# A hybrid encoder layer on one core: two backward states per step at the projection's end, and chunks beside the memory on the memory's PSUM banks

## The chip, the cores and the metric

The kernel runs on one core of one Trainium2 chip. The metric is the device time in microseconds (us) from start to end of one execution. A core has a TensorE (PE, matrix products into PSUM), a VectorE (DVE), a ScalarE (ACT), a GpSimd (POOL) and a SyncE (SP, which here issues most of the DMA loads); each works through its own queue in order, and semaphores tie the queues together.

## What is computed

One encoder layer in float32 for a sequence of 2048 rows of 1024 features, with 256 rows of memory:

```python
u = RMSNorm(x);  P = u @ w_in                 # one input projection
# Hyena group, 512 channels: short convolution, then two gated long convolutions
z = x1 * (h1 * z + d1 z);  z = x2 * (h2 * z + d2 z)      # filters as long as the sequence
# mLSTM group, 4 heads of 128: one scan forwards, one backwards, in chunks
s = (q @ k.T) * w;  num = s @ v + inter * (q @ C);  den = sum(s) + inter * (q @ n)
y += num / maximum(abs(den), exp(-m));  C = decay * C + (we * k).T @ v   # n likewise
x = x + concat(group_norm(z), group_norm(sigmoid(o) * y)) @ w_out
x = x + cross_attention(RMSNorm(x), RMSNorm(mem), wq, wk, wv, wo)        # 4 heads
x = x + relu(RMSNorm(x) @ w1) ** 2 @ w2;  return RMSNorm(x)
```

## The kernel before, in words

**Products.** The large products are three matmuls each on rounded parts of the operands: high by high, low by high and high by low (`mm3`, lines L355, L358, L359); `split` (L366) makes the parts with an ACT cast and a DVE subtraction. PSUM has eight banks of 2 KB per partition. Four carry the tag `mm` (method `mm`, L161) and take turns, four the tag `hy` (method `hy`, L164). A product that wants a bank waits until whoever read the bank four turns earlier has finished.

**The order.** The program is written as Python generators, each yielding a rough cost; `weave(a, b, wa, wb)` steps two generators so that their costs keep a ratio, `paced` and `among` put steps of one between steps of another. A scheduler, which simulates the engines, then decides the order of instructions on each engine; what it may reorder depends on data and on the turns of banks and buffers. So the written order, the set of banks and the buffers together set the queues.

**Stages.** First come the filters of the long convolution and the input projection (column sweeps `sweep`, row tiles `natural`), then the projection's rest woven with the convolution (`p.hyena`). Beside the projection's end run the mLSTM's gates and its *backward states*: the backward scan needs, for each of 16 chunks of 128 rows, the state that the later chunks leave, so `states`/`backward` walks from the last chunk to the first and stores the 15 states to memory (`cbd`). One step loads k and v (`L1178`, `L1184`), weights v, and in `update` (L1188) makes four matmuls (two to each of two banks, L1200) that DVE adds to the decayed old state (L1206).

The last stretch of the projection is `among(chain(sweep, natural), back, 1)`: one backward state after each step, and the remaining ones without anything between them.

Then follows the stage on which the change works, `chain(p.turned_in(), take(n, 1), beside_each(n, take(m, 5)))`:

- `n` is `memproj` (L693), the attention's work on the memory. `project` (L708) makes, for each of eight pairs, 16 products of the normed memory with a 256-column block of a weight; ACT copies the result to `kt` (L710). Then `keys` (L725, pairs 1 to 4) or `values` (L737, pairs 5 to 8) multiply it with a block of the next weight (16 or 8 products), ACT copies each bank to a buffer `o` and POOL's queue stores it (`gd`, `vw`). The weights `wm` come through SP (L415).
- `m` is `mlstm` (L1227). Its first step sets up and loads chunks 0 and 1, its next four are chunks 0 to 3. A chunk takes four score products (L1284, one bank), masks on POOL, an exponential on ACT (L1293) and a product on DVE (L1294); then for each direction eight products in two banks `pn` (L1322 with v, L1324 with the forward state `cf` or the stored backward state `cbn`), whose results ACT (L1327, L1336) and DVE (L1338) turn into the output `ht`; then `update` of the forward state. After every second chunk `bank_rsqrt` (L205) takes an inverse root on a PSUM bank with Newton steps (L213), which L1356 applies to the two chunks' rows. The other 12 chunks run later, woven into the attention.

The last part of the convolution also falls into this stage. For each of eight blocks SP loads transformed rows (`a<-zg`, two loads, L339) and the gate's rows (`a<-hy`, four loads, L974); PE makes the inverse transform's products (L173, L186), and the gated, normed rows are stored (`yh<-a`). The products of the transform before it are L987.

The *attention* stage starts with the loads of the mixed rows (`wn<-yh`, L1473), 16 transposes (L1479), a split, and the output projection (first matmul L355 with `act`) with columns of `w_out` (L1405).

In the generators the five steps of the mLSTM stand one behind each pair's step of the memory:

Of the kernel before, what the change touches and what calls it, by code (L numbers as in the profile page):

```python
# [128 lines left out]
class Prog:  # L129
    def __init__(self, ctx, tc, a):  # L130
        self.tc, self.nc, self.a = tc, tc.nc, a
        nc = self.nc
        self.ctx = ctx
        self.dr = ctx.enter_context(tc.tile_pool(name="dr", bufs=1, space=DRAM))
        self.s = {}
        cp = self.cp = ctx.enter_context(tc.tile_pool(name="cp", bufs=1))
        ident = cp.tile([128, 128], F32, name="ident")
        nc.gpsimd.memset(ident, 1.0)
        nc.gpsimd.affine_select(ident, ident, pattern=[[-1, 128]], compare_op=ALU.is_equal, fill=0.0,
                                base=0, channel_multiplier=1)  # L140
        self.ident = ident
        self.eps = cp.tile([128, 1], F32, name="eps")
        nc.vector.memset(self.eps, EPS)
        self.ones = cp.tile([128, 128], F32, name="ones")
        nc.vector.memset(self.ones, 1.0)
        self.flip = 0
        self.banks, self.strict = [], False
        self.pending = []
        self.prepq = None
        self.hooks, self.made, self.lag, self.rowb = {}, 0, [], None  # L150
        self.rbp = cp.tile([128, 16], F32, name="rbp")
        self.fb = cp.tile([128, 8], F32, name="fb")
        nc.scalar.activation(self.fb[:, 4:5], self.eps, AF.Copy)
        par = self.par = cp.tile([128, 192], F32, name="par")
        nc.scalar.dma_start(out=par, in_=a["par"])
        self.g_mix, self.g_mem, self.gx, self.gf = (par[:, 8 * i:8 * i + 8] for i in range(4))
        self.cw = par[:, 32:92].rearrange("p (i c) -> p i c", i=3)
        self.cb, self.gb = par[:, 92:112], par[:, 112:128]
        self.ps = ctx.enter_context(tc.tile_pool(name="ps", bufs=1, space=PSUM))
# [4 lines left out]
    def hy(self):  # L164
        t = self.ps.tile([128, 512], F32, tag="hy", name="hy", bufs=4)
        self.banks.append(t[:, 0:1].tensor.name)
        return t

    def beside(self, *products, pin=False):
        names = [p[0].tensor.name for p in products]  # L170
# [31 lines left out]
        else:  # L202
            self.nc.vector.tensor_copy(out, in_)

    def bank_rsqrt(self, pool, ss, n):  # L205
        nc, c = self.nc, ss.shape[1]
        m, ys = (pool.tile([128, c], F32, tag="br" + x, name="br" + x, bufs=2) for x in "my")
        nc.scalar.activation(m, ss, AF.Identity, bias=self.eps, scale=1.0 / n)
        b = self.hy()
        y, t = b[:, 0:c], b[:, 16:16 + c]  # L210
        nc.vector.tensor_scalar(y.bitcast(I32), m.bitcast(I32), -0.5, float(0x5F3759DF), ALU.mult, ALU.add)
        for _ in range(3):
            nc.vector.tensor_copy(ys, y)  # L213
            nc.vector.tensor_tensor(t, y, ys, ALU.mult)
            nc.vector.scalar_tensor_tensor(t, t, -0.5, m, ALU.mult, ALU.mult)
            nc.vector.scalar_tensor_tensor(y, t, 1.5, ys, ALU.add, ALU.mult)
        return y
# [970 lines left out]
    def update(self, sb, new, old, kk, va, r, eng, pin=None, bufs=2):  # L1188
        nc, pin = self.nc, pin or (lambda i: i)
        WC, DC = self.gcols[:, 2], self.gcols[:, 3]  # L1190
        ve = sb.tile([128, 4, 129], F32, tag="ve", name="ve", bufs=bufs) if bufs > 1 else va
        if eng is nc.scalar:
            for h in range(4):
                eng.activation(ve[:, h], va[:, h], AF.Copy, scale=WC[:, r + h:r + h + 1])
        else:
            eng.tensor_tensor(ve, va, WC[:, r:r + 4].unsqueeze(2).broadcast_to([128, 4, 129]), ALU.mult)
        for p in range(2):
            pc = self.hy()
            for i in range(2):
                pin(nc.tensor.matmul(pc[:, 129 * i:129 * i + 129], kk[:, 2 * p + i], ve[:, 2 * p + i], start=True, stop=True))  # L1200
            if old is None:
                nc.vector.tensor_copy(new[:, 2 * p:2 * p + 2].rearrange("d h e -> d (h e)"), pc[:, 0:258])
                continue
            for i in range(2):
                h = 2 * p + i
                nc.vector.scalar_tensor_tensor(new[:, h], old[:, h], DC[:, r + h:r + h + 1],  # L1206
                                               pc[:, 129 * i:129 * i + 129], ALU.mult, ALU.add)
# [19 lines left out]
    def mlstm(self, es):  # L1227
# [51 lines left out]

        def scores(n, ld):  # L1280
            qn, kk_t, cbn, va, rows_ = ld
            sp = self.hy().rearrange("p (h t) -> p h t", h=4)
            for h in range(4):
                nc.tensor.matmul(sp[:, h], kk_t[:, h], qn[:, h], start=True, stop=True)  # L1284
            for d in range(2):
                r = 64 * d + 4 * n
                nm = rows_[d, 0]
                if (d, 1) in rows_:
                    it = rows_[d, 1]
                    nc.gpsimd.tensor_tensor(it, it, qn, ALU.mult)  # L1290
                nc.gpsimd.tensor_tensor(nm, nm, masks[d].unsqueeze(1).broadcast_to([128, 4, 128]), ALU.add)
                for h in range(4):
                    nc.scalar.activation(nm[:, h], nm[:, h], AF.Exp, bias=GC[:, r + h:r + h + 1])  # L1293
                nc.vector.tensor_tensor(nm, nm, sp, ALU.mult)  # L1294
# [4 lines left out]
        for n in range(16):  # L1299
# [10 lines left out]
            for d in range(2):  # L1310
                r = 64 * d + 4 * n
                nm = rows_[d, 0]
                state = cf if d == 0 else cbn
                if d == 0:
                    y = sb.tile([128, 4, 128], F32, tag="h0", name="ht", bufs=2)
                pvs = []
                for p in range(2):
                    pn = self.hy()
                    for i in range(2):
                        h = 2 * p + i  # L1320
                        dst = pn[:, 129 * i:129 * i + 129]
                        nc.tensor.matmul(dst, nm[:, h], va[:, h], start=True, stop=state is None)  # L1322
                        if state is not None:
                            nc.tensor.matmul(dst, rows_[d, 1][:, h], state[:, h], start=False, stop=True)  # L1324
                    pvs.append(pn[:, 0:258].rearrange("t (h e) -> t h e", h=2))
                for p, pv in enumerate(pvs):
                    nc.scalar.activation(pn[:, 260 + 2 * p:262 + 2 * p].unsqueeze(2), pv[:, :, 128:129], AF.Abs)  # L1327
                den = sb.tile([128, 4, 1], F32, tag="den", name="den", bufs=4)
                dv = den.rearrange("t h o -> t (h o)")
                nc.vector.tensor_tensor(dv, pn[:, 260:264], EC[:, r:r + 4], ALU.max)  # L1330
                nc.vector.reciprocal(dv, dv)
                for p, pv in enumerate(pvs):
                    for i in range(2):
                        h = 2 * p + i
                        if d == 0:
                            nc.scalar.activation(y[:, h], pv[:, i, 0:128], AF.Copy, scale=dv[:, h:h + 1])  # L1336
                            continue
                        nc.vector.scalar_tensor_tensor(y[:, h], pv[:, i, 0:128], dv[:, h:h + 1], y[:, h], ALU.mult, ALU.add)  # L1338
# [10 lines left out]
                nc.scalar.activation(junk[:, h], y[:, h], AF.Square, accum_out=ss[:, c:c + 1])  # L1349
            ys.append(y)  # L1350
            if n % 2:
                rv = self.bank_rsqrt(sb, ss, 128)
                for i, y in enumerate(ys):
                    t0 = 128 * (n - 1 + i)
                    for h in range(4):
# [744 lines left out]
def program(p):  # L2100
    with ExitStack() as ms:
        with ExitStack() as es:
# [15 lines left out]
            with ExitStack() as hs:  # L2118
# [1 line left out]
                             p.natural(0, (3,)),  # L2120
                             paced(chain(p.sweep((4, 5, 8, 9), 0, False), p.natural(0, (0, 1))),
                                   p.gates(), back := p.states(), (0, 1) * 6 + (2,) * 6 + (2, 0)),
                             among(chain(p.sweep((6, 7), 0, False), p.natural(0, (2,), p.prep_mem, 2)), back, 1),
                             )
                weave(rest, p.hyena(hs), 445, 329)
            for _ in chain(p.turned_in(), take(n, 1), beside_each(n, take(m, 5))):
                pass
        with ExitStack() as rs:
            p.ts = rs.enter_context(ExitStack())
            p.tail_open(p.ts)  # L2130
# [10 lines left out]
def among(g, h, every):  # L2141
    for i, v in enumerate(g):
        yield v
        if i % every == every - 1:
            next(h, None)
    for _ in h:
        pass


def paced(g, h1, h2, plan):  # L2150
    for v, n in zip(g, plan):
        yield v
        if n:
            next((h1, h2)[n - 1], None)
    yield from g


def beside_each(g, h):
# [43 lines left out]
```

## Time and profile before

| | us |
|---|---|
| median of 3 runs | 3063.18 |
| lowest and highest run | 3056.71, 3065.72 |
| the profiled execution's own time | 3063.97 |
| its span in the profile | 3062.3 |
| PE busy | 2979.0 |
| DVE busy | 1953.2 |
| ACT busy | 1491.5 |
| POOL busy | 1263.4 |
| data moved by DMA | 607.03 MB, mean 198 GB/s |

The span is the time from the first to the last recorded instruction; the own time of the execution also holds what lies around it. Engine names and line numbers in the profile's rows are those of the kernel before. In a row of the timeline stand the start, the length, the engine, the line, the operation with output and input, the shape, the count, and in brackets the idle time just before with what ended it. Windows rows give the busy time of each engine in a stretch and the granted clock of PE. The mean granted clock over the whole span is 0.989.

### The profile page before, as it was taken

The numbers are of one execution on the slowest core, as the hardware profiler recorded it, in microseconds if no ns is written. First come the engines' busy times: TensorE is split into PE (matmuls) and PEld (weight loads), VectorE is DVE, ScalarE is ACT, GpSimd is POOL, SyncE is SP. The second block draws the span as 40 slices with busy tenths as digits, with TensorE's granted clock in tenths as the row PEclk, the third lists the DMA queues.
The fourth block names the chain that finished last, engine by engine and source line by source line (L and its number), as shares of the span: only waits on it lengthen the run. The fifth ranks groups of instructions, "written<-read, shape, count | busy, mean of one in ns | idle before, by whom it ended". The sixth has DMA issues, their size and how long they took to land.

```text
span 3062.3 us, 44144 instructions
## 1 busy us (share of the span) xinstructions
PE 2979.0 (97%) x14799; PEld 2367.6 (77%) x14799; DVE 1953.2 (64%) x3442; ACT 1491.5 (49%) x2930; POOL 1263.4 (41%) x1025
## 2 busy tenths in 40 slices
PE   9999999998999989999999999999999999999998
PEld 7666667775678867888888888888888888888876
DVE  8855464557755447867665666558555686566695
ACT  6443455634664235555544455556555543333335
POOL 0112113321443654333223247765665374344653
PEclk9999999999999999999999999999999999999999
DMA  6655676686877976463567466657544555444434
GB/s 223 197 186 170 213 263 214 192 273 216 279 229 221 348 265 198 149 228 125 196 202 264 137 219 217 208 178 250 190 151 152 196 192 169 118 157 121 155 103 165
DMA packets 423644, 607.03 MB, mean 198 GB/s; under 512 B 36847, under 2 KB 229999, under 8 KB 422393
## 3 DMA queue, kind: packets, MB, share of 16 engines
q1 hardware_dynamic: 395972, 525.42, 53.6%
q0 software_dynamic: 18992, 62.96, 5.6%
q10 hardware_dynamic: 8452, 15.83, 1.4%
q8 instruction: 117, 1.92, 0.3%
q14 instruction: 111, 0.90, 0.1%
HBM read 401.67 MB, written 202.41 MB: 197 GB/s over the span
## 4 chain that ended last, share of the span: by engine, by line
PE 58%; DVE 2%; DMA 1%; issue 1%; ACT 1%; POOL 0%; SPq 0%; DVEq 0%; POOLq 0%; ACTq 0%
PE mm L355 12%; PE mm L359 12%; PE mm L358 12%; PE hy L355 6%; PE hy L359 6%; PE hy L358 6%; PE hy L1322 1%; PE hy L1324 1%; DVE bl L1693 0%; PE hy L1284 0%; PE hy L1596 0%; DVE acc L1991 0%; PE hy L1200 0%; PE hy L1479 0%; DVE acc L2028 0%
## 5 line engine op out<-in xcount | busy, mean ns | idle before, releaser
L1692 ACT CAST ah<-w 128x512 fp32r<-128x512 f32 x284 | 176.6, 623 | 303.8 <-PE hy L358 150.2
L1693 DVE TENSOR_TENSOR bl<-wr,bh 128x512 fp32r<-128x512 f32 x213 | 240.3, 1132 | 126.5 <-ACT bh L1692 126.2
L366 DVE TENSOR_TENSOR wl<-wn,wh 128x512 fp32r<-128x512 f32 (+1 forms) x296 | 220.0, 787 | 89.2 <-ACT wh L366 89.2
L355 PE MATMUL mm<-xh,wh 128*128 128x512 f32 x640 | 264.5, 415 | 2.3 <-ACT xh L366 1.1
L358 PE MATMUL mm<-xl,wh 128*128 128x512 f32 x640 | 255.9, 400 | 5.5 <-DVE xl L366 5.4
L359 PE MATMUL mm<-xh,wl 128*128 128x512 f32 x640 | 254.5, 398 | 0.0
L1692 ACT CAST bh<-wr 128x512 fp32r<-128x512 f32 x232 | 143.4, 621 | 227.9 <-PE mm L359 169.5
L1693 DVE TENSOR_TENSOR al<-w,ah 128x512 fp32r<-128x512 f32 x236 | 216.5, 918 | 57.2 <-ACT ah L1692 56.9
L359 PE MATMUL mm<-bh,al 128*128 128x512 f32 x576 | 223.8, 391 | 3.4 <-DVE al L1693 3.4
L355 PE MATMUL mm<-bh,ah 128*128 128x512 f32 x576 | 225.9, 392 | 1.3 <-DVE acc L1854 1.1
L358 PE MATMUL mm<-bl,ah 128*128 128x512 f32 x576 | 224.9, 390 | 0.0
L366 ACT CAST wh<-wn 128x512 fp32r<-128x512 f32 (+1 forms) x296 | 164.3, 620 | 102.6 <-PE mm L359 51.1
L358 PE MATMUL mm<-act,wh 128*128 128x512 f32 x512 | 202.0, 395 | 0.0
L359 PE MATMUL mm<-act,wl 128*128 128x512 f32 x512 | 199.9, 392 | 0.0
L355 PE MATMUL mm<-act,wh 128*128 128x512 f32 x512 | 199.0, 395 | 0.6 <-ACT wh L366 0.5
L355 PE MATMUL hy<-bh,ah 128*128 128x512 f32 x448 | 175.2, 391 | 0.0
L358 PE MATMUL hy<-bl,ah 128*128 128x512 f32 x448 | 174.6, 390 | 0.0
L359 PE MATMUL hy<-bh,al 128*128 128x512 f32 x448 | 174.4, 390 | 0.0
L331 POOL TENSOR_TENSOR b<-b 128x512 f32<-128x512 f32 x32 | 48.1, 1504 | 293.6 <-DVE b L330 277.4
L355 PEld LDWEIGHTS mm<-xh,wh 128*128 128x128 f32 x640 | 121.1, 190 | 52.4 <-issue 18.7
L358 PEld LDWEIGHTS mm<-xl,wh 128*128 128x128 f32 x640 | 121.2, 189 | 50.9 <-issue 19.1
L355 PE MATMUL mm<-wh,xh 128*128 128x256 f32 (+1 forms) x512 | 155.7, 304 | 1.8 <-DVE a L960 1.8
(396 smaller groups left out, 8257.4 us busy)
## 6 DMA issues: line engine op xcount, KB each, us to landing
wr<-hc SPq DMA_DIRECT2D x224, 256.0 KB
w<-in_ff_w_dram SPq DMA_DIRECT2D x172, 256.0 KB
hc<-wn SPq DMA_DIRECT2D x128, 256.0 KB
wn<-in_w_in_dram SPq DMA_DIRECT2D x100, 256.0 KB
hc<-q SPq DMA_DIRECT2D x96, 256.0 KB
fs<-a SPq DMA_DIRECT2D x32, 512.0 KB
zs<-a POOLq DMA_DIRECT2D x32, 512.0 KB, 6.6
a<-fs SPq DMA_DIRECT2D x64, 256.0 KB
```

Of the source, the lines that this page charges most:

```text
L331: nc.gpsimd.tensor_tensor(b, f, b, ALU.subtract)
L355: first = mm(ps, lh, rh, start=start, stop=False)
L358: mm(ps, lh, rl, start=False, stop=False)
L359: self.last = mm(ps, ll, rh, start=False, stop=stop)
L366: both = (self.nc.scalar.copy(hi, src), self.nc.vector.tensor_tensor(lo, src, hi.bitcast(F32), ALU.subtract))
L1322: nc.tensor.matmul(dst, nm[:, h], va[:, h], start=True, stop=state is None)
L1324: nc.tensor.matmul(dst, rows_[d, 1][:, h], state[:, h], start=False, stop=True)
L1692: self.nc.scalar.copy(hi, src)
L1693: eng.tensor_tensor(lo, src, hi.bitcast(F32), ALU.subtract)
```

## The change

Two things are edited. In the projection's last stretch, `twice(back)` lets each step make two backward states instead of one. And while a flag `early` is set, which is during the memory stage alone, the mLSTM's scores, products, updates and the bank of the norm come from `mm()`, the set that the memory's products and the projection use, instead of `hy()`, the set that the convolution uses. Later chunks, in the attention, use `hy()` as before. The backward states of the last stretch still use `hy()` where the flag is not set.

```diff
+    def spare(self):
+        return self.mm() if self.early else self.hy()
...
-    def bank_rsqrt(self, pool, ss, n):
+    def bank_rsqrt(self, pool, ss, n, bank=None):
...
-        b = self.hy()
+        b = bank or self.hy()
...
-            pc = self.hy()
+            pc = self.spare()
...
-            sp = self.hy().rearrange("p (h t) -> p h t", h=4)
+            sp = self.spare().rearrange("p (h t) -> p h t", h=4)
...
-                    pn = self.hy()
+                    pn = self.spare()
...
-                rv = self.bank_rsqrt(sb, ss, 128)
+                rv = self.bank_rsqrt(sb, ss, 128, self.spare())
...
-                             among(chain(p.sweep((6, 7), 0, False), p.natural(0, (2,), p.prep_mem, 2)), back, 1),
+                             among(chain(p.sweep((6, 7), 0, False), p.natural(0, (2,), p.prep_mem, 2)), twice(back), 1),
...
+            p.early = True
             for _ in chain(p.turned_in(), take(n, 1), beside_each(n, take(m, 5))):
                 pass
+            p.early = False
...
+def twice(g):
+    for v in g:
+        yield v + next(g, 0)
```

Lines of the changed kernel are four higher in this part than those of before: L708 becomes L712, L725 L729, L737 L741, L173 L177, L186 L190, L1200 L1204, L1284 L1288, L1322 and L1324 L1326 and L1328, L1479 L1483, L339 L343, L974 L978.

On PE, at the start of the memory stage, the order before had a backward state (L1200 with `va`) or a block of the convolution (L173, L186) in each pair of the memory:

```order
L708 MATMUL mm<-mt,wm 128x256 x3
L1200 MATMUL hy<-va,kn 128x129 x4
L708 MATMUL mm<-mt,wm 128x256 x25
L173 MATMUL hy<-a,e_2743 32x512
L186 MATMUL hy<-a,e_2743 32x512 x7
L708 MATMUL mm<-mt,wm 128x256 x4
L725 MATMUL mm<-kt,wm 128x256 x16
L708 MATMUL mm<-mt,wm 128x256 x11
L1200 MATMUL hy<-va,kn 128x129 x4
```

The changed order at the same place, the first two pairs of the memory and the scores of the first chunks (L1288):

```order
L712 MATMUL mm<-mt,wm 128x256 x26
L177 MATMUL hy<-a,e_2743 32x512
L190 MATMUL hy<-a,e_2743 32x512 x7
L712 MATMUL mm<-mt,wm 128x256 x6
L729 MATMUL mm<-kt,wm 128x256 x16
L1288 MATMUL mm<-qn,kk_t 128x128 x4
...
L712 MATMUL mm<-mt,wm 128x256 x14
L729 MATMUL mm<-kt,wm 128x256 x12
L177 MATMUL hy<-a,e_2743 32x512
L190 MATMUL hy<-a,e_2743 32x512 x7
L729 MATMUL mm<-kt,wm 128x256 x4
L177 MATMUL hy<-a,e_2743 32x512
```

The states have moved ahead of the stage. Of the convolution's eight blocks three now stand ahead of the memory's first matmul (before, two), four stand in its first two pairs, and the eighth stands in the update of chunk 0; before, the last one stood behind the fifth pair.

On PE, at the end of the memory stage, the order before had the last value products (L737), then chunks 2 and 3 with nothing between, of which the start is shown, and after them the attention's transposes:

```order
L737 MATMUL mm<-wm,kt 128x512 x3
L1200 MATMUL hy<-ve,kn 128x129 x4
L1284 MATMUL hy<-qn,kk_t 128x128 x4
L1322 MATMUL hy<-va,rw 128x129
L1324 MATMUL hy<-cf,rw 128x129
```

In the changed order chunk 3's update is followed by two more pairs of the memory, and then by the transposes:

```order
L1204 MATMUL mm<-ve,kn 128x129 x4
L712 MATMUL mm<-mt,wm 128x256 x16
L741 MATMUL mm<-wm,kt 128x512 x8
L712 MATMUL mm<-mt,wm 128x256 x16
L741 MATMUL mm<-wm,kt 128x512 x16
L1483 MATMUL hy<-ident,wn 128x128 x16
L1288 MATMUL hy<-qn,kk_t 128x128 x4
```

Chunks 1 to 3 stand whole between pairs of the memory, each as one piece of 4 scores, 16 products and 4 update products, where before matmuls of the memory stood inside the pieces of chunks 0 and 1.

On SP's queue, the last blocks of the convolution (`a<-zg`, `a<-hy`) before, among the memory's weights:

```order
L1258 DMA cbn<-cbd 128x516 x2
L415 DMA wm<-in_xa_wo_dram 128x1024 x2
L415 DMA wm<-in_xa_wv_dram 128x4x256 x2
L339 DMA a<-zg_2739 128x1024 x2
L974 DMA a<-hy 32x1024 x4
L415 DMA wm<-in_xa_wo_dram 128x1024 x2
L415 DMA wm<-in_xa_wv_dram 128x4x256 x2
```

The same place in the changed order:

```order
L343 DMA a<-zg_2739 128x1024 x2
L978 DMA a<-hy 32x1024 x4
L419 DMA wm<-in_xa_wk_dram 128x4x256 x2
L419 DMA wm<-in_xa_wq_t_dram 128x1024 x2
L1263 DMA qn<-qt 128x4x128
L1263 DMA kk_t<-kt 128x4x128
L343 DMA a<-zg_2739 128x1024 x2
L978 DMA a<-hy 32x1024 x4
L419 DMA wm<-in_xa_wv_dram 128x4x256 x2
L343 DMA a<-zg_2739 128x1024 x2
L978 DMA a<-hy 32x1024 x4
L419 DMA wm<-in_xa_wq_t_dram 128x1024 x2
```

Ahead of the last block's loads there now stand 16 of the memory's weight items (the `x` counts of L419 in the whole queue), before 26 (L415).

More of the change, by code (lines that the diff above doesn't have):

```diff
@@ L135, in __init__ @@
         self.s = {}
+        self.early = False
         cp = self.cp = ctx.enter_context(tc.tile_pool(name="cp", bufs=1))
```

## The prediction

> **What bounds the kernel now.** I read the page first: its span, the busy shares of the engines and the clock.
>
> ```profile
> span 3062.3 us, 44144 instructions
> PE 2979.0 (97%) x14799; PEld 2367.6 (77%) x14799; DVE 1953.2 (64%) x3442; ACT 1491.5 (49%) x2930; POOL 1263.4 (41%) x1025
> ```
>
> TensorE (PE) is busy for 97% of the span; whatever else the change does, it can only win where PE waits or runs at a lower clock. The profiled execution took 3063.97 us with a span of 3062.3 us, so 1.7 us lie around the span, and it is 0.8 us above the median of the three runs, 3063.18 us. I make the sum as a difference and add it to the median.
>
> Next I cut the span by the windows view. Its columns are the length, the busy time of PE, weight load, DVE, ACT and POOL (with instruction counts), the granted PE clock, the DMA share and GB/s. The first row reaches from the first matmul of the memory projection to the first matmul of the output projection: the stretch on which the change works.
>
> ```profile
> core 0: us, PE busy (x) PEld busy (x) DVE busy (x) ACT busy (x) POOL busy (x), PEclk, DMA share, GB/s
> 997.07:1170.91 173.84, 155.37 (x794) 120.64 (x793) 87.59 (x281) 65.96 (x200) 105.30 (x118) 0.93 0.86 289
> 1020.00:1030.00 10.00, 9.30 (x39) 8.04 (x40) 5.16 (x17) 2.72 (x7) 6.47 (x7) 0.83 1.02 376
> 1140.00:1150.00 10.00, 4.84 (x19) 4.27 (x20) 8.69 (x36) 2.60 (x11) 4.98 (x6) 0.51 0.47 161
> 1150.00:1160.00 10.00, 8.93 (x59) 8.38 (x58) 7.24 (x26) 6.38 (x28) 6.37 (x6) 0.81 0.52 158
> 1160.00:1170.00 10.00, 4.60 (x25) 4.12 (x25) 6.07 (x23) 7.50 (x24) 2.15 (x2) 0.71 0.52 159
> ```
>
> PE misses 173.84 − 155.37 = 18.5 us of 173.84, and the four ten-microsecond windows show a clock well below 1. The timeline of PE shows where it waits; the last bracket is the idle time and what ended it. These are all the waits of the stretch.
>
> ```profile
> 997.07 1.46 PE L708 MATMUL mm<-mt,wm 128*128 128x256 f32 x6
> 1020.70 3.68 PE L725 MATMUL mm<-kt,wm 128*128 128x256 f32 x8 [2.36 <-ACT kt L710]
> 1134.20 1.13 PE L1284 MATMUL hy<-qn,kk_t 128*128 128x128 f32 x8 [1.60 <-issue]
> 1142.23 0.77 PE L1322 MATMUL hy<-va,rw 128*128 128x129 f32 x2 [5.12 <-DVE bry L213]
> 1145.10 0.80 PE L1322 MATMUL hy<-va,rw 128*128 128x129 f32 x2 [0.81 <-DVE ht L1356]
> 1149.31 2.09 PE L1200 MATMUL hy<-ve,kn 128*128 128x129 f32 x8 [2.12 <-ACT ht L1336]
> 1157.48 1.23 PE L1200 MATMUL hy<-ve,kn 128*128 128x129 f32 x8 [0.36 <-ACT ht L1336]
> 1159.41 0.66 PE L1479 MATMUL hy<-ident,wn 128*128 128x128 f32 x4 [0.70 <-DVE cf L1206]
> 1160.38 1.29 PE L1479 MATMUL hy<-ident,wn 128*128 128x128 f32 x8 [0.32 <-issue]
> 1166.72 1.12 PE L1479 MATMUL hy<-ident,wn 128*128 128x128 f32 x4 [5.04 <-DVE act L366]
> 1170.91 1.18 PE L355 MATMUL mm<-act,wh 128*128 128x512 f32 x4
> ```
>
> The brackets add up to 18.4 us. The largest, 5.12 us, stands in chunk 2 of the mLSTM, which comes after the last memory matmul: chunks 2 and 3 run bare there, and the bank that chunk 2's product wants is held by the norm of chunks 0 and 1 (L213, L1356). The other large one, 5.04 us, is the entry to the attention stage, between transposes.
>
> **The change part by part.** *What it can remove.* The idle time is 18.4 us. The clock costs busy time × (1 − granted clock): 9.30 × 0.17 = 1.6, 4.84 × 0.49 = 2.4, 8.93 × 0.19 = 1.7, 4.60 × 0.29 = 1.3 us, together 7.0. So 25.4 us can go at most, if chunks 1 to 3 stand among memory products and nothing is late there.
>
> *Work that only moves.* By the order of the changed kernel, the three backward states still left beside the memory, and one more block of the convolution's last inverse transform, stand ahead of the first memory matmul.
>
> ```profile
> 1028.97 1.05 PE L1200 MATMUL hy<-va,kn 128*128 128x129 f32 x8
> 1086.18 0.61 PE L173 MATMUL hy<-a,e 64*32 64x512 f32 x1
> 1087.20 7.17 PE L708 MATMUL mm<-mt,wm 128*128 128x256 f32 x32
> 1094.21 7.03 PE L737 MATMUL mm<-wm,kt 128*128 128x512 f32 x16
> ```
>
> A state is 0.9 us of PE (its matmuls start at 1028.97, the next group at 1029.86 in the same view), so three are 2.7 us; a convolution block goes from 1086.18 to 1087.20, 1.0 us. In front of the memory they cost the same 3.7 us that they no longer cost behind, and memory starts near 1000.8. I cost this at nothing: the projection's products (mm banks) cover the states' VectorE work there. Without that cover it is at most three waits of a state's chain, which I put at 0 to 3 us, with the nearest rows 0.36 and 0.70 above.
>
> *Given back (a): the chunks on the memory's banks.* Scores, both directions' products, updates and the norm's scratch now take turns with the memory's products in one set of four banks, and in the order each of chunks 1 to 3 is one unbroken piece (4 scores, 16 products, 4 updates), not threaded with memory matmuls. The next product waits until the bank four back is read. The nearest row below is chunk 3 of before, also unbroken: 0.36 + 0.70 = 1.1 us. The nearest above is chunk 2 of before, 5.12 + 0.81 + 2.12 = 8.1 us, where two norms stood in the way. Four chunks: 4 to 32 us. A memory pair of 7.17 + 7.03 us now stands between chunks, in which the norm can end, so I go near the lower row, twice it: 2.2 us for each of chunks 1 to 3 and 4 us for chunk 0, whose update is cut by a convolution block. That is 10.6 us.
>
> *Given back (b): the convolution's last blocks.* PE takes its queue in order; a convolution block whose rows have not landed stops the memory matmuls behind it. SP issues these loads, and its rows and the transfer sizes stand here.
>
> ```profile
> 958.68 0.80 SPq L339 DMA_DIRECT2D a<-zg  x2
> 1067.55 2.05 SPq L339 DMA_DIRECT2D a<-zg  x2
> a<-zg SPq DMA_DIRECT2D x16, 512.0 KB
> a<-hy SPq DMA_DIRECT2D x32, 128.0 KB
> wm<-in_xa_wq_t_dram SPq DMA_DIRECT2D x8, 512.0 KB
> gd<-o POOLq DMA_DIRECT2D x16, 256.0 KB, 7.5
> yh<-a POOLq DMA_DIRECT2D x32, 128.0 KB, 6.5
> va<-vd SPq DMA_DIRECT2D x11, 256.0 KB
> SPq L415 <- DMA a<-zg: 19.7, 11, 2.7
> core 0: us, PE busy (x) PEld busy (x) DVE busy (x) ACT busy (x) POOL busy (x), PEclk, DMA share, GB/s
> 970.00:1090.00 120.00, 117.64 (x695) 96.39 (x694) 61.77 (x168) 37.25 (x76) 74.45 (x86) 0.99 1.02 344
> 1030.00:1040.00 10.00, 10.00 (x59) 7.82 (x58) 3.51 (x8) 2.82 (x6) 7.46 (x11) 1.00 1.05 388
> ```
>
> The DMA engines are full here: share 1.02, 344 GB/s over 120 us; SP waits for landings of a<-zg 11 times. In before the last block is read at 1086.18 with no idle before it. In the changed order the seventh of the eight blocks stands behind two memory pairs: from 1000.8 come three projections (3 × 7.1), two key products (2 × 7.2), chunk 0's scores (1.0) and three blocks (3 × 1.0), hence PE is there near 1041. By SP's order there lie up to it 7 blocks of 2 × 512 + 4 × 128 KB (11.0 MB), 14 weight items of 512 KB (7.3), and some 5.3 MB of chunk loads and rows in 256 KB items, 23.6 MB; POOL's stores by then, about 8 of gd and 24 of yh, are 5.2 MB. The first of the loads, at 958.68 in before, comes about 11 us later in the changed order, as 40 more of the input projection's matmuls stand ahead of its releaser (at 1.46 / 6 = 0.24 us, the spacing in the row of 997.07, 10 us) and a state (0.9 us) with them: near 970. At 344 GB/s the 28.9 MB take 84 us, landing near 1054, 13 us late; at the 388 GB/s of the best window 74 us, 1044.5, 4 us late. I take 9 us, the middle; 0 to 18 as bounds (0 as SP may run ahead where the queue is in its favour, 18 with the eighth block, 1.6 MB of its own and 1 MB of weights, on top). The same count on before gives 41 MB from 958.7 at 344 GB/s, hence 1078, and PE came at 1086: the method agrees that nothing waits there.
>
> *Given back (c): the entry to attention.*
>
> ```profile
> 1128.97 2.74 PE L737 MATMUL mm<-wm,kt 128*128 128x512 f32 x6
> 1131.77 0.81 SPq L1473 DMA_DIRECT2D wn<-yh  x2
> ```
>
> The rows for attention are loaded at 1131.77, when the last memory matmul has just ended (1128.97 + 2.74 = 1131.71). Before, chunks 2 and 3 covered these loads; now PE goes from the last memory matmul straight to the transposes. I take 4 us, between 3 (a landing) and 8 (a landing plus the 5.04 us of the split). *(d) The clock.* One wait of 2.36 us stands before the 0.83 of the window 1020 to 1030, which cost 1.6 us. New waits as in (a) to (c), two or three of that size or more, cost 4 us; 2 to 6. The Trainium skill, "TensorE: Matmul & The Clock Gate", Part 1 (the HAM clock gate), puts the half clock behind an idle window of about 3.4 us; the row after 2.36 us is at 0.83 all the same, so here the measurement decides, and by the page's figure (d) would be some 2 us and the sum 2 us lower. *(e)* The convolution's first block needs the same 11 us later loads: 2 us, 0 to 4.
>
> Sum: 10.6 + 9 + 4 + 4 + 2 = 29.6 us back, less 25.4 removed: +4.2 us. On the median 3063.18 that is 3067 us. What a measurement of this kernel can tell from no change is about 0.3%, 9.2 us.
>
> **The rivals.** *R1, faster: the transfers do not bind.* SP's order puts the zg loads ahead of weights, so the blocks may land in time, b and e are 0, and chunks hide as chunk 3 did (a = 6). For it: 388 GB/s in one window; against it: 344 over 120 us. Back: 6 + 4 + 4 = 14, net −11.4, about 3052 us. The Trainium skill, "Perfetto Trace Analysis", Roofline, names about 435 GB/s as the ceiling of one core's DMA engines; at that estimate the 28.9 MB would take 66 us and no stall would be left, but no window here reached it.
>
> *R2, slower: PE stands at the convolution's last blocks.* SP's last zg load comes late, b is 18 and the wait puts the clock down (d = 6), and the chunk behind it restarts late: 10.6 + 18 + 5 + 6 + 2 = 41.6, net +16.2, about 3079 us. It decides from the point where the seventh block lands later than some 1059; at 344 GB/s that lacks 5 us. *R3, the change does not do what it says:* against it, the order shows mm banks in every chunk beside the memory and memory matmuls behind chunk 3. If bank turns simply move the same 18.4 us of idle, the time is that of no change, 3063; that lies inside the forecast's verdict.
>
> **How the numbers follow.** Forecast (within 0.3%) 0.5, with R3 0.03 beside it, together 0.53 for the same; R1 0.2; R2 and its neighbours (the bounds of a and c) 0.27. With a from 4 to 32 the ends alone would be wide, but they do not come together; the range reaches from R1's 3052 to a little past R2, 3082, and leaves out about 2 in 10. The likeliest case alone is 3058 to 3072.
>
> **What would show it.** Right: memory starts near 1001; no PE bracket of 5 us in chunks 1 to 3 and none behind L213; a wait of some 9 us at L177 (the line that L173 becomes) after the second key product; PE idle at the entry of 3 to 8 us with yh loads at memory's end. Wrong: the interval from memory's first to the projection's first matmul shorter by over 12 us, or no wait at L177 at all (then b falls and R1 is right); or idle before memory's own matmuls (L712, L729) with a chunk's ACT or DVE as releaser above 4 us a chunk (then a falls).

## The result and the profile after

The changed kernel takes 3089.24 us (median of 4 runs, 3086.3 to 3090.54), the kernel before 3064.45 us (4 runs): a ratio of 1.0084, 95% interval 1.0071 to 1.0097. It is 25 us slower; 3067 us had been forecast, with 3082 us as the upper end of the range.

The profiled execution has a span of 3088.8 us against 3062.3. First the same stretch as before, from the memory's first matmul to the output projection's first, and six pieces of it, in the windows view.

```profile
core 0: us, PE busy (x) PEld busy (x) DVE busy (x) ACT busy (x) POOL busy (x), PEclk, DMA share, GB/s
999.37:1193.08 193.71, 156.97 (x762) 120.05 (x761) 81.83 (x262) 66.29 (x199) 101.97 (x116) 0.89 0.79 257
1020.00:1030.00 10.00, 9.64 (x39) 7.91 (x40) 0.21 (x2) 2.71 (x8) 5.00 (x7) 0.80 1.05 312
1050.00:1060.00 10.00, 0.24 (x8) 0.26 (x16) 2.99 (x9) 1.26 (x3) 6.12 (x5) 0.56 1.07 303
1060.00:1070.00 10.00, 7.26 (x42) 5.15 (x27) 6.68 (x17) 2.13 (x8) 9.08 (x11) 0.67 1.03 388
1110.00:1120.00 10.00, 6.07 (x15) 4.92 (x16) 3.60 (x16) 0.58 (x1) 3.30 (x5) 0.52 0.33 129
1120.00:1140.00 20.00, 19.45 (x97) 14.70 (x96) 6.65 (x23) 9.38 (x33) 8.49 (x9) 1.00 0.71 233
1140.00:1160.00 20.00, 18.93 (x95) 14.24 (x94) 11.10 (x44) 9.30 (x34) 9.85 (x11) 1.00 0.71 234
```

The stretch is 193.71 us long, 19.9 more than before. The other 6.6 us of the span lie outside: its start is 2.3 us later, and what follows it is 4.3 us longer (1895.7 against 1891.4 us), without one wait that stands out. In the profiles of the experiments that follow the start lies between 995 and 1008 us, also where the kernels do the same up to there, so 2.3 us are within what one execution differs from another. The rear is another matter: in the nine experiments whose stretch ends as it does here it takes 1888.9 to 1891.3 us. The 4.3 us of the rear are spread over small waits, and their cause stays open.

Idle time is 193.71 − 156.97 = 36.7 us, twice the 18.5 of before. PE's timeline shows all of it but 1.7 us, which are four waits of 0.2 to 0.6 us:

```profile
1020.36 9.08 PE L729 MATMUL mm<-kt,wm 128*128 128x256 f32 x32 [5.79 <-DMA wm<-in_xa_wq_t_dram]
1045.03 0.59 PE L177 MATMUL hy<-a,e 64*32 64x512 f32 x1 [1.39 <-DMA a<-zg]
1059.76 1.03 PE L177 MATMUL hy<-a,e 64*32 64x512 f32 x1 [11.71 <-DVE hy L220]
1068.01 0.52 PE L1326 MATMUL mm<-va,rw 128*128 128x129 f32 x2 [2.13 <-ACT ht L1340]
1093.29 1.23 PE L1204 MATMUL mm<-ve,kn 128*128 128x129 f32 x8 [0.36 <-ACT ht L1340]
1095.35 7.17 PE L712 MATMUL mm<-mt,wm 128*128 128x256 f32 x32 [0.84 <-DVE cf L1210]
1113.93 6.47 PE L729 MATMUL mm<-kt,wm 128*128 128x256 f32 x16 [7.95 <-DVE ht L1360]
1145.52 1.23 PE L1204 MATMUL mm<-ve,kn 128*128 128x129 f32 x8 [0.36 <-ACT ht L1340]
1147.45 7.17 PE L712 MATMUL mm<-mt,wm 128*128 128x256 f32 x32 [0.70 <-DVE cf L1210]
1185.90 4.12 PE L1483 MATMUL hy<-ident,wn 128*128 128x128 f32 x16 [3.77 <-DMA wn<-yh]
```

The waits that the change was aimed at are gone: chunks 2 and 3 stand between memory matmuls, with waits of 0.2 to 0.7 us, and of the 5 us waits of the stage's end 3.77 us at the first transposes are left. Three long waits have come instead, and the clock with them.

*The second weight, 5.79 us.* The first key product wants `wq`. (The kernel before waits 2.36 us at the same place, there put down to ACT's copy of `kt`.) SP's rows, the changed kernel and then the kernel before:

```profile
1002.66 1.25 SPq L343 DMA_DIRECT2D a<-zg  x2
1005.95 4.27 SPq L978 DMA_DIRECT2D a<-hy  x4
1010.51 2.58 SPq L419 DMA_DIRECT2D wm<-in_xa_wq_t_dram  x2
```

```profile
1001.17 2.73 SPq L415 DMA_DIRECT2D wm<-in_xa_wq_t_dram  x2
```

A fifth block of the convolution's rows is now issued ahead of the weight, which comes 9 us later.

*The seventh block of the convolution, 11.71 us.* The page names a VectorE instruction as the releaser, but the matmul waits for several semaphores, and that instruction is a step in the middle of the sixth block's norm, which frees no bank and which the matmul doesn't need. It needs the rows whose second load SP issues at 1048.55:

```profile
1048.55 1.50 SPq L343 DMA_DIRECT2D a<-zg  x1
```

PE starts 9.7 us after that issue is over. The experiments below have the same wait with `DMA a<-zg` as the releaser (12.20 and 11.37 us), and it goes when the rows are halved.

*The norm of chunks 0 and 1, 7.95 us.* The norm's bank now belongs to the memory's set, and a key product wants it. The rows of ACT show why the norm is late; below them stands VectorE's row of the norm's application, behind which the key product starts:

```profile
1104.90 1.14 ACT L370 CAST wh<-we 128x512 fp32r<-128x512 f32 x2 [4.33 <-DMA we<-in_w_out_dram]
1107.13 1.12 ACT L370 CAST wh<-we 128x512 fp32r<-128x512 f32 x2
1108.15 0.30 ACT L212 ACTIVATE brm<-ss,eps 128x8 f32<-128x8 f32 x1
1108.36 0.56 ACT L714 COPY kt<-mm 128x512 f32<-128x512 f32 x1
```

```profile
1111.65 2.22 DVE L1360 SCALAR_TENSOR_TENSOR ht<-ht,mm,gml 128x128 f32<-128x128 f32 x8
```

ACT's queue stands 4.33 us at a cast of the output projection's first columns, whose load has not landed. The squares of the norm, its first step on their sums (L212), and the memory's own copies (L714) stand behind that cast.

*The clock.* The same work at full clock would be 148.4 − 3.7 = 144.7 us (before's 155.37 less its 7.0 of clock, less the moved work); PE was busy for 157.0, so the clock takes some 12.3 us. Added up as the prediction did it, busy time × (1 − granted clock) over ten-microsecond windows, it is 11.0. The windows at 1050, 1060 and 1110, behind the two long waits, have 0.56, 0.67 and 0.52. The Trainium skill, "TensorE: Matmul & The Clock Gate", section "A second HAM failure mode: psum-queue depth-cycling" in Part 1, tells of another kernel, in bf16, in which frequent short idle times between groups of products that take turns in PSUM banks made the clock swing. This trace doesn't show it: with the waits of 0.2 to 0.7 us of chunks 2 and 3 in the memory's banks, 1120 to 1160 stayed at 1.00, and every ten-microsecond window of the stretch below 0.9 lies at a wait of 3.8 us or more.

### The profile page after: what moved, and what is told of

It is laid out like the page before. It is cut to its first block, busy times and chain, and to the rows that moved or that the text cites. A ratio compares the mean times of both kernels' runs of the same rounds, so it can differ in the third digit from the quotient of the medians.

```text
span 3088.8 us, 44136 instructions
## 1 busy us (share of the span) xinstructions
PE 2984.4 (97%) x14799; PEld 2368.5 (77%) x14799; DVE 1935.9 (63%) x3442; ACT 1493.6 (48%) x2930; POOL 1260.4 (41%) x1025
## 3 DMA queue, kind: packets, MB, share of 16 engines
q8 instruction: 117, 1.92, 0.3%
## 4 chain that ended last, share of the span: by engine, by line
PE 59%; DMA 5%; DVE 3%; issue 1%; POOL 1%; SPq 0%; ACT 0%; DVEq 0%; ACTq 0%; POOLq 0%
PE mm L359 12%; PE mm L362 12%; PE mm L363 12%; PE hy L363 6%; PE hy L359 6%; PE hy L362 6%; DMA a<-hy 1%; PE mm L712 1%; PE mm L741 1%; PE hy L1326 1%; PE hy L1328 1%; DMA va<-vd 1%; PE mm L729 0%; PE hy L1483 0%; DVE bl L1697 0%
## 5 line engine op out<-in xcount | busy, mean ns | idle before, releaser
L370 DVE TENSOR_TENSOR wl<-wn,wh 128x512 fp32r<-128x512 f32 (+1 forms) x296 | 212.8, 763 | 88.8 <-ACT wh L370 88.6
```

The lines of the kernel that those rows point to most:

```text
L370: both = (self.nc.scalar.copy(hi, src), self.nc.vector.tensor_tensor(lo, src, hi.bitcast(F32), ALU.subtract))
```

## The experiments

Twelve kernels were run. Three theories stood at the start: **A**, that the loss is the convolution's last rows and the memory's weights crowded together, which DMA can't bring sooner, because the chunks have left the convolution's banks; **B**, that the states, which have moved ahead, crowd them; **C**, that it is the chunks' turn in the memory's banks, the norm's above all. The ratios are against the kernel before, run beside them on the same chip. The twelve ran in three groups on three chips, on which the kernel before took 3063.2, 3063.9 and 3059.4 us, so ratios are compared between groups.

| run | median us | ratio | 95% interval |
|---|---|---|---|
| states only | 3065.31 | 1.0005 | 0.9994 to 1.0016 |
| banks only | 3081.34 | 1.0053 | 1.0037 to 1.0068 |
| norm on the convolution's banks | 3086.15 | 1.0071 | 1.0059 to 1.0084 |
| half rows | 3074.26 | 1.0035 | 1.0023 to 1.0047 |
| chunks later | 3084.80 | 1.0063 | 1.0049 to 1.0078 |
| states only, chunks later | 3061.32 | 0.9994 | 0.9984 to 1.0004 |
| no early columns | 3078.90 | 1.0048 | 1.0035 to 1.0061 |
| states only, spread blocks | 3063.51 | 1.0004 | 0.9996 to 1.0013 |
| half rows and no early columns | 3066.87 | 1.0018 | 1.0009 to 1.0027 |
| products on the convolution's banks | 3087.97 | 1.0087 | 1.0074 to 1.0100 |
| products alone on the memory's banks | 3092.14 | 1.0098 | 1.0085 to 1.0111 |
| states only, rows early | 3065.26 | 1.0012 | 1.0001 to 1.0022 |

**States only.** The flag is never set.

```diff
-            p.early = True
+            p.early = False
```

> Only the two backward states per step; every chunk keeps the convolution's banks (the flag is never set). Theory A (the loss is the convolution's last loads and the memory's second weight crowded together at the memory's start, and that crowding comes from the chunks' products leaving the hy banks, which lets blocks of the convolution run next to each other): the five blocks stand spread over the first five pairs again, no wait over 5 us at L177, time near before or better, 3050 to 3066. Theory B (the crowding comes from the states having moved ahead, so that the fifth block's loads stand ahead of the second weight on SP's queue, which is so here too): the waits at L729 for the weight and at L177 for zg stay, 3078 or more. Theory C (the loss is the chunks' turn in the memory's banks, the norm's above all): no 8 us wait before L729, 3055 to 3070, with the waits for weights and zg still there.

It is as fast as before, as theory C had it: 3055 to 3070 us, no 8 us wait before L729, and the waits for data still there. PE's rows:

```profile
1024.34 9.37 PE L729 MATMUL mm<-kt,wm 128*128 128x256 f32 x32 [4.83 <-DMA wm<-in_xa_wq_t_dram]
1062.26 1.03 PE L177 MATMUL hy<-a,e 64*32 64x512 f32 x1 [5.43 <-DMA a<-zg]
1129.33 0.49 PE L1326 MATMUL hy<-va,rw 128*128 128x129 f32 x2 [3.63 <-DVE ht L1360]
```

So the two states per step bring a crowding of loads (4.8 us for the weight, 9.1 at L177 in all), as theory B said, and they also pay for it: the chunks end beside the memory, and of the waits of the stage's end 3.63 us behind the norm and 4.2 us at the first transposes are left. In this kernel chunks are threaded with memory matmuls. B's 3078 is refuted. A's time holds, but not its sign, no wait over 5 us at L177; the seventh block's wait is halved (11.71 to 5.43 us) and not gone.

**Banks only.**

```diff
-    among(chain(...), twice(back), 1),
+    among(chain(...), back, 1),
```

> Only the change of banks; one backward state per step. Three states stand in the memory again, and the convolution's last blocks spread a little further, up to chunk 1's update. Theory A (crowded loads): as slow as both together or a little less, 3078 to 3090, with a wait at L177 of 5 to 15 us. Theory B (the states ahead crowd it): near before, 3058 to 3068. Theory C (bank turns): the 8 us wait of L729 behind the norm stays, 3070 to 3085, with no long wait at L177.

3081 us: the banks alone cost 16 to 18 us, whether or not the states move. The times of A and of C both hold; A's wait of 5 us or more at L177 isn't there, and C's 8 us behind the norm are 3.75. There is no long wait, but a row of smaller ones, 4.30 (a chunk's product behind the convolution's norm on VectorE), 4.71 (L177), 3.75 (the norm) and 4.99 us (a product behind ACT).

**The norm on the convolution's banks.**

```diff
-                rv = self.bank_rsqrt(sb, ss, 128, self.spare())
+                rv = self.bank_rsqrt(sb, ss, 128)
```

> Both parts, but the norm's scratch bank stays in the convolution's set; PE's order is almost that of the changed kernel. Theory C1 (the norm's bank holds up the memory's key product at 1106 to 1114): the 7.95 us before L729 are gone and the clock with it, 3077 to 3081. Theory C2 (ACT's queue is stuck behind the cast of the output projection's columns that wait for their load, and the copies of the memory's own banks stand behind that cast too): a wait of 3 to 6 us stays there with ACT as releaser, 3083 to 3087. Theory A takes no side on this wait; the waits for zg (13 us) and the weight (6 us) stay by it.

It gains 3 to 4 us, though its interval and that of the whole change overlap. In PE's rows the wait before L729 is gone, and one of the same size stands later:

```profile
1058.33 1.03 PE L177 MATMUL hy<-a,e 64*32 64x512 f32 x1 [12.20 <-DMA a<-zg]
1123.50 2.09 PE L1204 MATMUL mm<-ve,kn 128*128 128x129 f32 x8 [8.58 <-ACT ht L1340]
```

```profile
1122.82 1.14 ACT L1340 ACTIVATE ht<-mm,den 128x128 f32<-128x128 f32 x4 [3.33 <-DMA ym<-ht]
```

Chunk 2's output takes the buffer of chunk 0's (there are two), which is free only when the norm has been applied and stored. So C1, the bank alone, falls; C2 is nearer, with its 3083 to 3087: the norm is late, and whoever needs its result next, by a bank or by a buffer, waits.

**Half rows.** Each block of the convolution's last pass loads one of its two row tiles and uses it twice (half of that transform's input is left out).

```diff
-            r = [ta() for h in range(2)]
-            for h in range(2):
+            r = [ta() for h in range(2 - o)]
+            for h in range(2 - o):
                 self.by_phase(nc.sync, gds[o], j2, h, r[h], True)
+            r = (r + r)[:2]
```

> Both parts, but each block of the convolution's inverse transforms in the last pass loads one of its two row tiles and uses it for both (half of the transform's input is left out): 0.5 MB less a block, 3.7 MB up to the seventh block, at 344 GB/s 10.7 us. PE's order stays close. Theory A (DMA decides): the 11.7 us at L177 fall to 0 to 3, the 5.8 us for the weight to 0 to 3, with some of the clock back: 3066 to 3073. Theory C (banks, the norm, ACT) as the whole cause: 3085 or more.

3074 us, 15 us less, one microsecond above A's range, and far from the 3085 of C as the whole cause. Of 13.1 us at L177 inside the stretch none is left, and the wait for the weight is 2.5 us. A is right on this part: the seventh block waited for data, and 3.7 MB fewer ahead of it end that. What the same edit would gain in the kernel before wasn't run.

**No early columns.**

```diff
-            nxt = self.columns(items.pop(0), lambda: A.tile([128, 512], F32, tag="e", name="we", bufs=4))
+            nxt = self.columns(items.pop(0))
```

> Both parts, but the output projection's first columns use the common staging buffers, so that their loads and casts no longer stand in ACT's queue beside the memory. PE's order is that of the changed kernel. Theory C2 (the 7.95 us of L729 behind the norm come from ACT and DVE standing at the cast of those columns until their load lands): this wait falls to 0 to 2, with 1 to 2 us of clock; the entry of attention pays 3 to 10 us for the later columns; 3082 to 3094 in all. Theory C1 (the norm is late of itself, as in the kernel before where 5.1 us stood there): 5 us or more stay.

3079 us, 10 us less. PE's row behind the norm:

```profile
1109.43 5.41 PE L729 MATMUL mm<-kt,wm 128*128 128x256 f32 x16 [1.92 <-DVE ht L1360]
```

7.95 us have become 1.92, though the norm still uses a memory bank: the cast in ACT's queue made it late, as C2 said. C2's time, 3082 to 3094, was too high, because the entry of attention paid half a microsecond (4.2 us at the first transposes against 3.8). Here too the edit wasn't made to the kernel before. With the states alone ACT stands at the same cast, the norm's first step comes 16 us behind it in that kernel (1123.8), and PE has no wait in these 16 us:

```profile
1107.28 0.62 ACT L370 CAST wh<-we 128x512 fp32r<-128x512 f32 x1 [4.90 <-DMA we<-in_w_out_dram]
```

So the late cast costs PE time only where something that PE needs next stands close behind it.

**Both at once.** The two edits above together.

> Both parts of the change, with both suspected costs taken away at once: half of the rows for each block of the convolution's last pass (half of that transform's input is left out) and the output projection's first columns in the common staging buffers. Alone the first gave 15 us and the second 10 us of the 25. If they are two separate costs: 3062 to 3068, no loss left. If they are one cost seen twice (a PE that stands makes the next thing late): 3070 to 3076.

3067 us, 1.0018: of 25 us some 5 are left. The two savings, 15 and 10 us alone, give 20 together, so they are mostly separate costs.

**Chunks later, with both kinds of banks.** The memory goes three steps ahead before the chunks start; in the first run with the whole change, in the second with the flag never set. The convolution's blocks stand at the same places in both.

```diff
-            for _ in chain(p.turned_in(), take(n, 1), beside_each(n, take(m, 5))):
+            for _ in chain(p.turned_in(), take(n, 3), beside_each(n, take(m, 5))):
```

> Both parts, and the memory goes three steps ahead before the chunks start, instead of one. PE's order: the convolution's blocks stand in the memory's first three pairs with projections between them (the seventh about 6 us of matmuls later than in the changed kernel), and chunks 0 to 3 as unbroken pieces on the memory's banks behind them. Theory A (PE comes too early to the convolution's rows, which DMA can't bring sooner): the wait at L177 falls from 11.7 us to 4 to 7, that for the second weight stays at 4 to 6, time 3070 to 3080. Theory C (the chunks' turn in the memory's banks is the loss): the time stays at 3084 to 3090, since the chunks still take those banks as whole pieces.

> As the run with the chunks later, but with the chunks on the convolution's banks (states only). The convolution's blocks and SP's loads stand as in that run up to the eighth block; the chunks are threaded with the memory's matmuls. What differs is the banks alone. Theory A: the waits at L177 and for the weight are as there; the time is lower only by what the unbroken pieces cost (2 to 4 us). Theory C: lower by 8 us or more, because no memory product waits for a chunk's bank; 3055 to 3066.

The windows of the two, from the memory's first to the projection's first matmul (eight products of chunk 4 stand ahead of the latter in the first, 1190.31 to 1193.61, and behind it in the second):

```profile
1004.72:1193.61 188.89, 160.12 (x763) 122.15 (x761) 84.90 (x266) 65.93 (x200) 102.27 (x116) 0.91 0.80 264
```

```profile
996.43:1158.92 162.49, 147.66 (x746) 113.22 (x745) 77.93 (x252) 63.37 (x197) 101.12 (x114) 0.96 0.89 299
```

The waits for rows are 9.3 and 6.9 us, those for the weight 4.6 and 4.3, and still the medians differ by 23 us. C had both times (3084 to 3090 and 3055 to 3066), A neither its 3070 to 3080 nor its 2 to 4 us between the two. So A isn't the whole cause: what the banks cost does not need the convolution's bunching. The first run has two further long waits of PE; below them stand rows of ACT:

```profile
1080.38 9.47 PE L712 MATMUL mm<-mt,wm 128*128 128x256 f32 x32 [4.55 <-issue]
1124.11 0.80 PE L1326 MATMUL mm<-va,rw 128*128 128x129 f32 x2 [4.81 <-ACT mm L1331]
```

```profile
1123.47 0.59 ACT L719 COPY o<-mm 128x512 f32<-128x512 f32 x1 [6.21 <-DMA vw<-o]
1123.95 0.35 ACT L1331 ACTIVATE mm<-mm 128x2 f32<-128x2 f32 x2
```

The first has no releaser in the profile, and what it waits for stays open. For the second the rows show it. The memory's copies go to three buffers that are stored to DRAM, and ACT waits for a store to land; the chunk's step L1331 stands behind that copy in ACT's queue, and PE behind both. In the second run ACT waits as long for a store, and PE has no wait at all from 1063 to 1149:

```profile
1067.03 0.59 ACT L719 COPY o<-mm 128x512 f32<-128x512 f32 x1 [6.90 <-DMA gd<-o]
```

There memory matmuls stand between the chunk's products and cover it. Whether more buffers for `o` would remove the wait wasn't tried.

**States only, spread blocks.** As the second run with the chunks later, with fewer buffers for the convolution's rows.

```diff
-            return sb.tile([128, 2, CH], F32, tag="a", name="a", bufs=10)
+            return sb.tile([128, 2, CH], F32, tag="a", name="a", bufs=8)
```

> States only, the memory three steps ahead, and 8 instead of 10 buffers for the convolution's rows, which puts the memory's second weight ahead of half of the fifth block's loads on SP and spreads the convolution's last five blocks over four pairs of the memory. Theory A (crowded loads decide): the wait for the second weight falls to 0 to 2 us, those at L177 to 0 to 5 in all, and with the chunks threaded among the memory's matmuls the time falls below both kernels, 3046 to 3056. If it stays at 3060 to 3068, the same waits come back elsewhere (loads late because of fewer buffers) and what bounds this stage is the amount of data.

3063.5 us, no gain. The weight's wait is 2.4 us, but L177 still waits 8.3 us in all and the first transposes 4.8. By the expectation's own terms, it is the amount of data; with it goes that in the 60 us from 1000 on the DMA share is 1.0 in every variant, before and after too. A run with less data in this kernel, which would show it, wasn't made.

**Which products on which banks.** In the first run the sixteen products (`pn`) stay in the convolution's set, in the second they alone are in the memory's. The edit of the first:

```diff
-                    pn = self.spare()
+                    pn = self.hy()
```

> Both parts, but the chunks' sixteen products stay in the convolution's banks; scores, updates and the norm are on the memory's. PE's order is that of the changed kernel up to the seventh convolution block, the eighth one stands in the memory's third key product, and chunks 0 and 1 follow each other there. Theory A (the seventh block comes before its rows have landed): 9 to 12 us at L177 stay, 3076 to 3088. Theory F (it is the products on the memory's banks that bunch chunks and blocks): the wait falls under 5 us, 3064 to 3072.

> Both parts, but only the chunks' sixteen products are on the memory's banks; scores, updates and the norm on the convolution's. The seventh and the eighth block stand directly behind each other after the second key product. Theory A: PE waits for the eighth block's rows too, 15 to 25 us at L177 in all, 3080 to 3095. Theory F: as slow as the whole change, 3084 to 3092, but from waits of the products on ACT and DVE.

1.0087 and 1.0098: each half of the bank change is as slow as the whole. In the first, 11.48 us stay at L177, as A expected. In the second, the seventh and the eighth block come right behind each other and both wait:

```profile
1059.94 1.03 PE L177 MATMUL hy<-a,e 64*32 64x512 f32 x1 [9.41 <-DMA a<-zg]
1071.37 1.03 PE L177 MATMUL hy<-a,e 64*32 64x512 f32 x1 [9.46 <-DMA a<-zg]
```

F, which blames the products alone, falls in the first.

**States only, rows early.** From the second run with the chunks later; the first four row tiles take the buffers of the early columns, the columns the common ones.

```diff
...
-            yn = self.stage()
+            yn = A.tile([128, 512], F32, tag="e", name="yn", bufs=4) if first else self.stage()
...
```

> States only, the memory three steps ahead, and the attention's first four row tiles loaded into the buffers that the output projection's first columns had, the columns into the common ones. The 5.2 us at the first transposes (rows that are loaded only when the memory's buffers are free) go; the first matmul of the output projection then waits for its columns, 2 to 5 us. If the two loads are the same wait in turn: as the run without it, 3058 to 3064; if the columns come sooner than the rows did: 3054 to 3059.

3065 us, no gain: the 5.2 us at the first transposes are gone, and 1.57 us there, 2.64 in the output projection's first products, 3.13 at chunk 4's update and 2.16 at a later transpose have come. None of the twelve is clearly faster than the kernel before.

## Why the prediction was wrong, point by point

*What bounds the stage* was right: PE waits, with the clock behind them, and the change took the waits of chunks 2 and 3 and most of those of the stage's end away. The run with the states alone shows that the banks were not needed for that, up to 3.63 us behind the norm.

*"25.4 us can go at most, if ... nothing is late there"* was booked in full, and something was late. The sum has no term for the second weight, which costs 5.8 us; the prediction followed SP's queue for the convolution's rows and not for the weight behind them.

*(a) Chunks on the memory's banks, 10.6 us, 4 to 32:* 14.0. The chunks' own nine waits are 6.1 us, less than was forecast; the norm adds 7.95. The prediction said that a memory pair now stands between chunks, "in which the norm can end"; this step failed, because ACT's queue stood at the cast of the columns, which the working never listed among the things that the change moves. It goes back to how the 5.12 us of before were read. The bank of the norm was said to hold them up, and VectorE's rows say otherwise:

```profile
1140.81 1.28 DVE L1294 TENSOR_TENSOR rw<-rw,hy 128x512 f32<-128x512 f32 x2
1142.82 2.22 DVE L1356 SCALAR_TENSOR_TENSOR ht<-ht,hy,gml 128x128 f32<-128x128 f32 x8
```

PE goes on at 1142.23, right behind the end of L1294 (1142.09), which reads a chunk's scores and stands in VectorE's queue between the steps of the norm; the norm's own bank is read by L1356 until 1145.04, and only the 0.81 us that follow belong to it. So even then a late step in a queue set the wait, and a change of bank could not end it.

*(b) The convolution's last blocks, 9 us, 0 to 18:* 13.1 us, 11.7 of it at the seventh block, as foreseen. The count of bytes gave 1054 as the landing and 1041 for PE; PE came at 1048 and the rows near 1059. The bytes were right: 29.3 MB were moved from the first load's issue to the block's start, against 28.9, and 14 weight items lie ahead of the block's loads, as counted. (Ahead of the last block's loads in the kernel before the trace has 24 and not 26.) The loads began at 965 and not at 970, and the rate was 311 and not 344 GB/s. The mechanism was right and the size within its bounds.

*(c) The entry, 4 us:* 3.8 at the first transposes. *(e) The first block, 2 us:* 3.0.

*(d) The clock, 4 us, 2 to 6:* 12.3 (11.0 by the prediction's own way). This is the step that missed by most, and the only one outside its bounds. It was taken from one wait of 2.36 us, but waits of 6, 8 and 12 us stood in the changed kernel.

With what was measured: 14.0 + 13.1 + 3.8 + 12.3 + 3.0 + 5.8 = 52.0 us come back against 25.4 removed, +26.6, where the forecast had +4.2. Of the 22.4 us between them the clock has 8.3, the weight 5.8, (b) 4.1, (a) 3.4, and (c) and (e) together 0.8. The span grew by 26.5. That the two agree so well is partly luck: the start came 4.4 us sooner than the moved work and the first block's wait make it, and the rear took 4.3 us longer, both unexplained. R2 had the place, and its condition, a landing later than some 1059, was just met; it named two thirds of the price. Its stall (18) was too large, its clock (6) too small, and it had no weight, so its 3079 us, and with it the range, fell short of 3089.

*The cause.* Shown: without the bank change there is no loss (states alone 1.0005), with it alone there is most of it (1.0053), and with both all (1.0084), so the states add to it only where the banks are shared. About 15 us of it hang on the rows of the convolution's last blocks and 10 on the early columns' cast, 20 together; that the kernel before would gain nothing from the same two edits is assumed and not shown. The states alone bring crowded loads as well and pay for them. That banks of one set are taken in the order in which the program asks for them, so that a chunk written behind a memory pair can't be threaded with the next pair's products, is read from PE's order in the two kernels with the chunks later; it fits all runs, but no run tests it by itself. How the last 5 us divide, and how far the full buffers of the memory's output add to them, stays open.

## What to carry to other kernels

In this kernel, work that fills the gaps of other work did worse when it took turns with it in one set of banks: the chunks were threaded with memory matmuls as long as they had another set, and stood as whole pieces when they had not. When a wait is booked as removed, ask which late instruction it waited for, and look for that one in the new order too; a bank moves the wait, and only the late instruction ends it. And where a step runs at a DMA share of 1.0, count what is issued ahead of each load before work is packed more closely.

## What the runs showed of the hardware that was not expected

The profile's releaser can be wrong for a wait on several semaphores: the same wait at the seventh block is put down to `DVE hy L220` (11.71 us), `DVE hy L219` (11.48) and `DMA a<-zg` (12.20, 11.37) in kernels where the same load is late. One wait of 7.95 us left 0.52 of the clock in the ten microseconds around its end, while the windows with chunk waits of 0.2 to 0.7 us stood at 1.00.
